# A gated hybrid decoder block on one core: gate scalings, a weight conversion, two row blocks of the output projection and one prepared product change their places

## The chip, the core and the metric

The kernel runs on one NeuronCore of a Trainium2 chip. Its engines work side by side, each on its own queue of instructions: TensorE (PE in the profile, with PEld for its weight loads), VectorE (DVE), ScalarE (ACT), GpSimd (POOL) and SyncE (SP), which here issues the DMA transfers. The metric is the time of one execution in device microseconds (us).

## The reference

One decoder layer on 1024 rows of 1024 numbers in float32, with two attention branches whose outputs are gated and added, a projection, and a gated feed-forward part:

```python
h = rmsnorm(x, mix_norm_g[l])
proj = h @ w_in[l]
qa, ka, va, q_lat, kv_lat, k_r, g_a, g_b = jnp.split(proj, IN_OFFSETS, axis=-1)
...
y = jax.nn.sigmoid(g_a) * (o_a @ w_o_swa[l]) + jax.nn.sigmoid(g_b) * (o_b @ w_o_mla[l])
x = x + y @ w_out[l]
h = rmsnorm(x, ffn_norm_g[l])
x = x + (jax.nn.silu(h @ w_gate[l]) * (h @ w_up[l])) @ w_down[l]
return rmsnorm(x, final_norm_g)
```

`o_a` comes from a sliding-window attention and `o_b` from a latent attention, each with 8 heads of 64.

## The kernel before

**Products in three parts.** Every float32 operand is split into a high part (a cast to the reduced type `fp32r`, made by ScalarE) and a low part (the difference, made by VectorE). `split` (L161) writes both. A product is then three matmuls per 128 of depth (`mm3`, L168): high by high (L172), high by low (L173), low by high (L174). So a product can begin when the cast is there, and its third matmul needs VectorE's subtraction as well.

**Seven products in place of eight.** The gate projection (`g_a`, `g_b`) and the feed-forward products are done by the class `Seven` (L710). It works through pairs `j` of weight columns; for each pair it makes seven products `q` in the order 1, 6, 2, 7, 5, 4, 3 out of sums and differences of weight quarters and of row quarters. A pair's raw weights come in two halves `kh` of the depth. For the next pair, `run` (L789) does at given products: the loads, the scaling of the gate weights by the norm's gain (`scale_part`, L739, four pieces `k` per half, done by ScalarE in `scale_gate`, L831), and the `mix` (L750), in which GpSimd makes the sums. `prep` (L764) makes the high and low part (`wl`) of a product's weights; `n_ahead` says how many products ahead of its use (3 for the gates).

**The gates run inside the sliding-window attention.** The loop at L1025 goes over 16 query blocks; each does three gate products and in between the block's transposes, scores and sums. TensorE and SyncE keep the written order there; the order of ScalarE, VectorE and GpSimd is made by a planner that runs ahead of the chip with its own picture of costs, after the written order as priority. GpSimd has the sums' denominators (`den`, L935) and the scaling of the probabilities in the same queue as the mix.

**The mixing loop** (L1444) goes over eight column tiles `dc` in the order 4, 5, 0, 1, 6, 7, 2, 3. Tile number `i` loads what later tiles need, takes the sigmoids of the next tile (L1429), and in `mix_b` (L1411) makes the product `oB` with the MLA output weights in two halves, in PSUM buffers of which there are four; VectorE multiplies each half by its gate (L1420), adds, and splits the result into `yh` and `yl`. The output weights come in pairs (`ob`, in the order 2, 0, 3, 1), each used by two tiles, and are converted by `conv_to`: pair 3 at the end of tile 2, for use in tile 4. Small SBUF tiles share 21 buffers. From L1043 up to the fourth segment of the next loop, every engine's order is the planner's.

**The output projection** (L1611) goes through four segments (`seg`) of four row blocks `b`. Each block adds 24 matmuls (8 column tiles of `y` by three) in one PSUM buffer, `xo`, and VectorE adds the result to `x`.

**Start of the feed-forward part.** From segment 3 on (L1613) the order of TensorE, VectorE, ScalarE and GpSimd is the written one. Products are called one by one (L1654 on), and between them stand `prep_to(n)`, which prepares the weights of all products before number `n`, and the late parts of the transposed rows (`rest`, L1498: casts `b22h`, `t3h`, and four subtractions).

Of the kernel before, what the change touches and what calls it, by code (L numbers as in the profile page):

```python
# [21 lines left out]
NK = D // P  # L22
# [67 lines left out]
def hybrid_block_kernel(  # L90
# [49 lines left out]
    def uid(name):  # L140
        counter[0] += 1
        return f"{name}_{counter[0]}"

    def U(name, dt=F32, shape=(P, 1024)):
        return pool.tile(list(shape), dt, tag="u", name=uid(name))
# [4 lines left out]
    def tiny(name, w=1):  # L150
        return small.tile([P, w], F32, tag=f"t{w}", name=uid(name))

    def P1(name, shape=(P, 512)):
        return ps1.tile(list(shape), F32, tag="ps", name=uid(name))

    def PX(name, shape=(P, 512)):
        return psum["x"].tile(list(shape), F32, tag="ps", name=uid(name))
# [10 lines left out]
    def mm3(ps, pairs, first=True, last=True, go_on=False):  # L168

        n = len(pairs)  # L170
        for i, ((ah, al), (bh, bl)) in enumerate(pairs):
            nc.tensor.matmul(ps, ah, bh, start=first and i == 0, stop=False, skip_group_check=go_on)  # L172
            nc.tensor.matmul(ps, ah, bl, start=False, stop=False, skip_group_check=go_on)  # L173
            nc.tensor.matmul(ps, al, bh, start=False, stop=last and i == n - 1, skip_group_check=go_on)  # L174
# [4 lines left out]
    def add(out, a, b, eng):  # L179
        eng.tensor_tensor(out, a, b, op=ALU.add)  # L180

    def blk(b, n=1):
        return slice(b * P, (b + n) * P)

    def half(s):
        return slice(512 * s, 512 * s + 512)
# [32 lines left out]
    st = Stream()  # L219
# [89 lines left out]
    def rstd_of(ss, width, r=None):  # L309
        ms = tiny("ms")  # L310
        nc.gpsimd.tensor_scalar(ms, ss, 1.0 / width, EPS, op0=ALU.mult, op1=ALU.add)  # L311
        if r is None:
            r = tiny("rstd")
        nc.gpsimd.tensor_tensor(r, ms, neg_half, op=ALU.pow)  # L314
        return r
# [6 lines left out]
    def hT(k, sl):  # L322
        hi, lo = quad[(k // 4, sl.start // 512)]
        c = slice(sl.start % 512, (sl.stop - 1) % 512 + 1)
        return hi[:, k % 4, c], lo[:, k % 4, c]

    def load_x(b):
        t = U("x")
        nc.sync.dma_start(t, x[blk(b), :])
        return t  # L330
# [188 lines left out]
    ps = kvq_ps[0] = PX("kvq")  # L519
# [334 lines left out]
        for d, t in late:  # L854
            nc.sync.dma_start(d, t)

    gates = Seven(NK, "g", load_gate, gate_done, 3, (1, 6), 5, scale=scale_gate, scale_at=[(2, 0, 0, 2), (7, 0, 2, 2), (7, 1, 0, 2), (5, 1, 2, 2)], piece=2, vec=(2, 5))

    def sw_q(it):
        qn = U("qn")  # L860
# [3 lines left out]
    for b in range(NB):  # L864
# [4 lines left out]
        ps = PX("ql", (P, 416))  # L869
# [109 lines left out]
    for i, b in enumerate((4, 5, 6, 7, 0, 1, 2, 3)):  # L979
        ps = P1("kl", (P, KVL))  # L980
# [184 lines left out]
    ob = {}  # L1165
# [110 lines left out]
    def mix_a(dc, sh, c0, n, ps=None):  # L1276
        if ps is not None:
            oa_ps[(dc, sh)] = ps
        ps = oa_ps[(dc, sh)]
        if (sh, c0) == (0, 0):  # L1280
            if dc < 4:
                ar[dc] = U("ar")
            elif dc % 2 == 0:
                t = V("ar", F32, (P, 2, S))
                ar[dc], ar[dc + 1] = t[:, 0], t[:, 1]
            if dc % 2 == 0:
                wo[dc // 2] = st.get(("oa", dc // 2))
        w = wo[dc // 2]
        mm3(ps, [((w[0][:, c, blk(dc % 2)], w[1][:, c, blk(dc % 2)]), oaT[(c, sh)]) for c in range(c0, c0 + n)],
            c0 == 0, c0 + n == 4)  # L1290
        if c0 + n == 4:
            nc.scalar.copy(ar[dc][:, half(sh)], oa_ps.pop((dc, sh)))
            if sh == 1 and dc < 4:
                nc.sync.dma_start(ar_d[dc], ar.pop(dc))
# [16 lines left out]
    DCS = (4, 5, 0, 1, 6, 7, 2, 3)  # L1311

    def load_sigs(dc):
        for i in (dc, 8 + dc):
            load_sig(i)
        if dc < 4:
            ar[dc] = U("ar")
            nc.sync.dma_start(ar[dc], ar_d[dc])
# [92 lines left out]
    def mix_b(dc, i):  # L1411
        if dc % 2 == 0:
            wo[4 + dc // 2] = st.get(("ob", dc // 2))
        w = wo[4 + dc // 2]
        ga, gb = gate.pop(dc), gate.pop(8 + dc)
        for sh in range(2):
            cs = half(sh)
            pb = PX("oB")
            mm3(pb, [((w[0][:, c, blk(dc % 2)], w[1][:, c, blk(dc % 2)]), obT[(c, sh)]) for c in range(4)])
            nc.vector.tensor_tensor(gb[:, cs], pb, gb[:, cs], op=ALU.mult)  # L1420
            if i == 7:
                add(ga[:, cs], ga[:, cs], gb[:, cs], nc.vector)
                split(*hT(dc, cs), ga[:, cs])
        for sh in range(2 if i < 7 else 0):
            cs = half(sh)
            add(ga[:, cs], ga[:, cs], gb[:, cs], nc.vector)
            split(*hT(dc, cs), ga[:, cs])

    def sigmoids(dc):  # L1429
        for i in (dc, 8 + dc):  # L1430
            sigmoid(i)
        a_ = ar.pop(dc)
        for sh in range(2):
            nc.gpsimd.tensor_tensor(gate[dc][:, half(sh)], a_[:, half(sh)], gate[dc][:, half(sh)], op=ALU.mult)
# [9 lines left out]
    for i, dc in enumerate(DCS):  # L1444
        if i in (1, 2):
            st.load_to(st.index[("ob", (3, 1)[i - 1])])
        if 2 <= i < 6:
            st.load_to(st.index[("out", 0, OUT0[i - 2])])
        if i + 2 < 8:
            load_sigs(DCS[i + 2])  # L1450
        if rest:
            mix_a(*rest.pop(0), 0, 4, PX("oA"))
        if i + 1 < 8:
            sigmoids(DCS[i + 1])
        mix_b(dc, i)
        if i in (2, 3):
            st.conv_to(st.index[("ob", (3, 1)[i - 2])])
        if i >= 4:
            st.conv_to(st.index[("out", 0, OUT0[i - 4])])

# [60 lines left out]
    def ffn_done(j, m, ps, f, sh, other):  # L1521
# [8 lines left out]
        else:  # L1530
# [3 lines left out]
    ffn = Seven(HF, "gu", load_w, ffn_done, 4, (2, 7), 5, head,  # L1534
                {(1, 6): [("load", 2, 0)], (1, 7): [("load", 2, 1)], (1, 5): [("mix", 2)]})
# [75 lines left out]
    for seg, (sh, hf) in enumerate(((0, 0), (0, 1), (1, 1), (1, 0))):  # L1611
        if seg == 3:
            in_order.__enter__()  # L1613
        if seg in (0, 1, 3):
            r = {0: 0, 1: 1, 3: 2}[seg]
            wo2 = [st.get(("out", r, j)) for j in range(4)]
        hs = half(hf)
        for b in range(4 * sh, 4 * sh + 4):
            if seg in (0, 2):
                x2[b] = load_x(b)  # L1620
            if (seg, b) == (2, 4):
                ffn.load_part(0, 0)
            if (seg, b) == (2, 6):
                ffn.load_part(0, 1)
            if (seg, b) == (2, 7):
                ffn.mix(0)
            ps = P1("xo")
            mm3(ps, [(hT(k, blk(b)), (wo2[k // 2][0][:, k % 2], wo2[k // 2][1][:, k % 2])) for k in DCS])
            add(x2[b][:, hs], ps, x2[b][:, hs], nc.vector)
            if seg in (0, 2):  # L1630
                st.conv_to(st.index[("out", seg // 2 + 1, b % 4)])
            if seg in (1, 3):
                xn = U("xn")
                ss = tiny("ss")
                nc.scalar.activation(xn, x2[b], AF.Square, accum_out=ss)  # L1635
                rs = rstd_of(ss, D)
            lower = to_h(*prev) if prev is not None else None
            prev = None
            if seg in (1, 3):
                nc.vector.scalar_tensor_tensor(xn, x2[b], rs, fg_bc, op0=ALU.mult, op1=ALU.mult)  # L1640
                prev = (xn, b)
                if (seg, b) == (3, 6):
                    ffn.prep_to(3)
                nc.sync.dma_start(x2_d[b], x2.pop(b))
            if (seg, b) == (3, 7):
                for kh in range(2):
                    ffn.load_part(1, kh)
            if lower is not None:
                if seg == 3 and b >= 6:
                    late_parts.append(lower)  # L1650
                else:
                    lower()
# [1 line left out]
    ffn.run()  # L1654
    late_parts.pop(0)()
    ffn.run()
    ffn.prep_to(4)
    late_parts.pop(0)()
    ffn.run()
    ffn.prep_to(6)  # L1660
# [89 lines left out]
    i = 0  # L1750
# [125 lines left out]
```

## Time and profile before

| | us |
|---|---|
| median of three runs | 1347.35 |
| lowest, highest | 1344.85, 1347.43 |
| the profiled execution, its own time | 1345.58 |
| its span, first to last instruction | 1343.8 |
| TensorE busy in the span | 1325.5 |
| VectorE, ScalarE, GpSimd busy | 903.5, 635.7, 567.6 |

The span is taken by the hardware profiler; the execution's time holds some 2 us around it. In the time line each row has its start, its length, engine, line, operation and the tiles written and read; in brackets stands how long the engine was idle before it, and what ended that. A row of the table of waits has the total, the number of times and the longest. A helper such as `split` or `mm3` gives all of its instructions one line, so the tiles tell them apart.

### The profile page before, as it was taken

The page shows a single profiled execution, that of the slowest core. Times are in us where ns is not written, and L with a number is a line of the kernel's source. Part 1 is how long each engine was busy: PE and PEld are TensorE (multiplying, and loading weights), DVE is VectorE, ACT ScalarE, POOL GpSimd, SP SyncE. Part 2 cuts the span into 40 slices and gives each one's busy share as a digit, 9 for nine tenths or more (in the row PEclk, how much of TensorE's full clock was granted, in tenths as well). Part 3 has the DMA queues.
Part 4 walks back from the last instruction along what each step waited for, and adds up shares of the span by engine and source line. Part 5 has one row for each costly group of instructions (what it writes and reads, how often), then busy time and mean ns, then how long its engine had stood idle before and what let it go on. Part 6 is the DMA issues. An engine that isn't in the chain of part 4 may idle for free. (4 is left out here: it accounts for less than half of the span.)

```text
span 1343.8 us, 19035 instructions
## 1 busy us (share of the span) xinstructions
PE 1325.5 (99%) x6564; PEld 1115.0 (83%) x6564; DVE 903.5 (67%) x1471; ACT 635.7 (47%) x1291; POOL 567.6 (42%) x614
## 2 busy tenths in 40 slices
PE   9999999999999999999999999999999999999997
PEld 6899878888888889877887888888888888888886
DVE  7868777776767667696458775566665664764862
ACT  7434767665556767762436223232223232644343
POOL 2116646553224554451031665756666541022521
PEclk9999999999999999999999999999999999999999
DMA  9454322335476430771432454545544425996504
GB/s 374 152 188 156 118 97 83 109 124 187 155 243 160 107 99 17 264 268 48 190 140 96 166 175 146 203 162 180 177 141 153 164 96 194 383 373 238 173 13 144
DMA packets 85311, 223.61 MB, mean 166 GB/s; under 512 B 9632, under 2 KB 16288, under 8 KB 84128
## 3 DMA queue, kind: packets, MB, share of 16 engines
q1 hardware_dynamic: 83776, 220.05, 47.5%
q10 hardware_dynamic: 1440, 2.36, 0.5%
q8 instruction: 52, 0.85, 0.3%
q14 instruction: 43, 0.35, 0.1%
HBM read 151.72 MB, written 70.12 MB: 165 GB/s over the span
## 5 line engine op out<-in xcount | busy, mean ns | idle before, releaser
L166 DVE TENSOR_TENSOR wl<-wr,wl 128x512 fp32r<-128x512 f32 x150 | 150.8, 1029 | 72.6 <-ACT wl L163 72.2
L166 DVE TENSOR_TENSOR lrv<-lr,lrv 128x1024 fp32r<-128x1024 f32 x77 | 105.1, 1396 | 49.3 <-ACT lrv L163 45.3
L163 ACT CAST lrv<-lr 128x1024 fp32r<-128x1024 f32 x77 | 80.1, 1052 | 95.7 <-PE fd L174 69.8
L172 PE MATMUL fd<-lrv 128*128 128x512 f32 x308 | 119.8, 389 | 0.0
L173 PE MATMUL fd<-lrv 128*128 128x512 f32 x308 | 119.8, 389 | 0.0
L174 PE MATMUL fd<-lrv 128*128 128x512 f32 x308 | 119.8, 389 | 0.0
L177 POOL TENSOR_TENSOR wr<-wr,sm 128x512 f32<-128x512 f32 (+1 forms) x38 | 46.2, 1225 | 145.4 <-DVE wl L166 114.2
L163 ACT CAST wl<-wr 128x512 fp32r<-128x512 f32 x150 | 86.9, 622 | 1.9 <-DVE wr L835 1.7
L1198 POOL TENSOR_TENSOR denb<-denb,neg_one 128x1 f32<-128x1 f32 x64 | 40.1, 626 | 96.2 <-ACT p L1197 84.1
L166 DVE TENSOR_TENSOR wl<-sm,wl 128x512 fp32r<-128x512 f32 x60 | 48.7, 837 | 46.3 <-ACT wl L163 46.2
L311 POOL TENSOR_SCALAR ms<-ss 128x1 f32<-128x1 f32 x32 | 9.4, 292 | 143.7 <-ACT xn L1635 67.5
L173 PEld LDWEIGHTS fd<-lrv 128*128 128x128 f32 x308 | 57.8, 188 | 12.1
L174 PEld LDWEIGHTS fd<-lrv 128*128 128x128 f32 x308 | 57.8, 188 | 12.0
L172 PEld LDWEIGHTS fd<-lrv 128*128 128x128 f32 x308 | 57.8, 188 | 11.9
L1197 ACT ACTIVATE p<-scb,nmb 128x384 f32<-128x384 f32 (+3 forms) x64 | 47.8, 747 | 33.3 <-DVE nmb L1196 25.6
L166 DVE TENSOR_TENSOR ptl<-pTb,pth 128x512 fp32r<-128x512 f32 (+2 forms) x96 | 50.5, 552 | 16.6 <-ACT pth L163 16.3
L1196 DVE CUSTOM_DVE_ANT_0 scb<-scb,mask 128x384 f32<-128x384 f32 (+3 forms) x64 | 48.6, 761 | 15.0 <-PE scb L1188 13.0
L1529 ACT ACTIVATE act<-sm 128x512 f32<-128x512 f32 x11 | 7.0, 633 | 104.8 <-DVE sm L180 104.8
L1199 POOL TENSOR_SCALAR p<-p,denb 128x384 f32<-128x384 f32 (+3 forms) x64 | 47.9, 748 | 6.3
L172 PE MATMUL xo<-wv,yh 128*128 128x512 f32 x120 | 47.4, 395 | 1.2 <-ACT yh L163 1.2
L1529 ACT ACTIVATE act<-pu 128x512 f32<-128x512 f32 x22 | 13.9, 633 | 71.0 <-DVE pu L180 71.0
L163 ACT CAST pth<-pTb 128x512 fp32r<-128x512 f32 (+2 forms) x96 | 43.4, 482 | 8.5 <-PE pTb L1213 7.5
(356 smaller groups left out, 4315.1 us busy)
## 6 DMA issues: line engine op xcount, KB each, us to landing
lr<-la_d SPq DMA_DIRECT2D x77, 256.0 KB, 5.4
wr<-in_w_gate_dram SPq DMA_DIRECT2D x22, 512.0 KB, 4.4
wr<-in_w_up_dram SPq DMA_DIRECT2D x22, 512.0 KB, 5.1
wd<-in_w_down_dram SPq DMA_DIRECT2D x22, 512.0 KB, 7.1
rb_d<-wd SPq DMA_DIRECT2D x22, 512.0 KB, 2.7
la_d<-sd SPq DMA_DIRECT2D x22, 512.0 KB, 5.9
lr<-rb_d SPq DMA_DIRECT2D x44, 256.0 KB, 5.4
lr<-in_w_down_dram SPq DMA_DIRECT2D x33, 256.0 KB, 5.4
```

Source lines behind the costliest of these rows:

```text
L163: i = nc.scalar.copy(hi, src)
L166: (eng or nc.vector).tensor_tensor(lo, src, hi.bitcast(F32), op=ALU.subtract)
L172: nc.tensor.matmul(ps, ah, bh, start=first and i == 0, stop=False, skip_group_check=go_on)
L173: nc.tensor.matmul(ps, ah, bl, start=False, stop=False, skip_group_check=go_on)
L174: nc.tensor.matmul(ps, al, bh, start=False, stop=last and i == n - 1, skip_group_check=go_on)
L177: eng.tensor_tensor(out, a, b, op=ALU.subtract)
L311: nc.gpsimd.tensor_scalar(ms, ss, 1.0 / width, EPS, op0=ALU.mult, op1=ALU.add)
L1196: nc.vector.tensor_tensor_reduce(s_, s_, m_, 1.0, -NEG, op0=ALU.add, op1=ALU.min, accum_out=nm)
L1197: nc.scalar.activation(p_, s_, AF.Exp, scale=-1.0, bias=nm, accum_out=den)
L1198: nc.gpsimd.tensor_tensor(den, den, neg_one[:, 0:1], op=ALU.pow)
L1199: nc.gpsimd.tensor_scalar(p[:, 0:w], p[:, 0:w], den, 0.0, op0=ALU.mult, op1=ALU.add)
L1529: nc.scalar.activation(dst, src, AF.Silu)
```

## The change

Four places change; no arithmetic is added or left out.

1. In the gates, the last two pieces of the next pair's first half are scaled at product 2 in place of product 7, and the last two of its second half at product 7 in place of product 5.
2. In the mixing loop, the fourth weight pair in number (`ob` 3) is converted at the end of tile 1 in place of tile 2. Pair 1 stays at the end of tile 3.
3. In the first segment of the output projection, blocks 0 and 1 get their PSUM buffers together. The first six column tiles are summed for block 0, then for block 1, then the last two for block 0, and for block 1.
4. In the feed-forward part, product 4 is prepared together with product 3, ahead of the second late part and of product 2.

```diff
-    ... scale_at=[(2, 0, 0, 2), (7, 0, 2, 2), (7, 1, 0, 2), (5, 1, 2, 2)], piece=2, vec=(2, 5))
+    ... scale_at=[(2, 0, 0, 2), (2, 0, 2, 2), (7, 1, 0, 2), (7, 1, 2, 2)], piece=2, vec=(2, 5))
...
         mix_b(dc, i)
-        if i in (2, 3):
-            st.conv_to(st.index[("ob", (3, 1)[i - 2])])
+        if i in (1, 3):
+            st.conv_to(st.index[("ob", (3, 1)[i // 2])])
...
-            ps = P1("xo")
-            mm3(ps, [(hT(k, blk(b)), (wo2[k // 2][0][:, k % 2], wo2[k // 2][1][:, k % 2])) for k in DCS])
+            if seg == 0 and b < 2:
+                if b == 0:
+                    xo2 = [P1("xo") for _ in range(2)]
+                    for ks in (DCS[:6], DCS[6:]):
+                        for u in range(2):
+                            mm3(xo2[u], [(hT(k, blk(u)), (wo2[k // 2][0][:, k % 2], wo2[k // 2][1][:, k % 2])) for k in ks],
+                                ks[0] == DCS[0], ks[0] != DCS[0])
+                ps = xo2[b]
+            else:
+                ps = P1("xo")
+                mm3(ps, [(hT(k, blk(b)), (wo2[k // 2][0][:, k % 2], wo2[k // 2][1][:, k % 2])) for k in DCS])
             add(x2[b][:, hs], ps, x2[b][:, hs], nc.vector)
...
     late_parts.pop(0)()
     ffn.run()
-    ffn.prep_to(4)
+    ffn.prep_to(5)
     late_parts.pop(0)()
     ffn.run()
     ffn.prep_to(6)
```

More of the change, by code (lines that the diff above doesn't have):

```diff
@@ L855, in gate_step @@
             nc.sync.dma_start(d, t)
-    gates = Seven(NK, "g", load_gate, gate_done, 3, (1, 6), 5, scale=scale_gate, scale_at=[(2, 0, 0, 2), (7, 0, 2, 2), (7, 1, 0, 2), (5, 1, 2, 2)], piece=2, vec=(2, 5))
+    gates = Seven(NK, "g", load_gate, gate_done, 3, (1, 6), 5, scale=scale_gate, scale_at=[(2, 0, 0, 2), (2, 0, 2, 2), (7, 1, 0, 2), (7, 1, 2, 2)], piece=2, vec=(2, 5))
     def sw_q(it):
```

## The prediction

> **What bounds the kernel now.** I read the head of the page first, then the table of TensorE's waits, then the time line around each wait.
>
> ```profile
> span 1343.8 us, 19035 instructions
> PE 1325.5 (99%) x6564; PEld 1115.0 (83%) x6564; DVE 903.5 (67%) x1471; ACT 635.7 (47%) x1291; POOL 567.6 (42%) x614
> ...
> PE fa L172 <- ACT wl L163: 3.3, 3, 1.5
> PE xo L172 <- ACT yh L163: 1.2, 1, 1.2
> ```
>
> TensorE (PE) is busy for all but 18.3 us of the span, so only its stops can give anything. The table names few: three waits of the gate and feed-forward products (`fa`) for a converted weight (`wl`), 3.3 us together, and one of the output projection (`xo`) for the mixed rows (`yh`). The time line places them, with two more on `oB`, the product with the MLA output weights. The bracket is PE's idle time and what ended it.
>
> ```profile
> 197.68 0.50 PE L172 MATMUL fa<-hh,wl 128*128 128x512 f32 x1 [1.04 <-ACT wl L163]
> ...
> 276.76 0.50 PE L172 MATMUL fa<-hh,wl 128*128 128x512 f32 x1 [0.76 <-ACT wl L163]
> ...
> 587.09 0.50 PE L172 MATMUL oB<-obT,wh 128*128 128x512 f32 x1 [0.94 <-ACT wh L163]
> ...
> 589.40 0.50 PE L174 MATMUL oB<-obT,wl 128*128 128x512 f32 x1 [0.89 <-DVE wl L166]
> ...
> 616.32 0.50 PE L172 MATMUL xo<-wv,yh 128*128 128x512 f32 x1 [1.24 <-ACT yh L163]
> ...
> 716.92 0.39 PE L174 MATMUL fa<-b21h,wl 128*128 128x512 f32 x1
> 718.77 0.50 PE L172 MATMUL fa<-b11h,wl 128*128 128x512 f32 x1 [1.46 <-ACT wl L163]
> ...
> 719.50 0.50 PE L174 MATMUL fa<-b11h,wl 128*128 128x512 f32 x1
> 719.84 0.40 PE L172 MATMUL fa<-b11h,wl 128*128 128x512 f32 x1
> ```
>
> A stop costs more than its bracket. In the last one four steps take 719.84 - 716.92 = 2.92 us. Undisturbed, matmuls of this shape start 0.227 us apart (a row quoted further down, at 727.79, is the 35th after that at 719.84), so four take 0.91 and the twelve of a product 2.72. The stop costs 2.01 us: 1.46 idle and 0.55 more, since the third matmul needs the low part that VectorE (DVE) makes after ScalarE's (ACT) cast. I put 0.55 on each stop, once on the pair at 587 and 589, where the two halves are late one after the other: 1.59 and 1.31 (gates), 2.38 (`oB`), 1.79 (`xo`), 2.01 (feed-forward). That is 9.08 us, all that this change can reach.
>
> **Gate weights.** The four scaling pieces of a gate pair's second half (`kh` 1) and the four of its first half now hang on one product each; two of each half move one product up. Nothing is added or removed: 56 scalings of one kind before and after. What must move is the cast that PE waits for at 197.68.
>
> ```profile
> 175.78 1.71 ACT L837 ACTIVATE wr<-wr,gT 128x256 f32<-128x256 f32 x4
> ...
> 181.50 0.47 ACT L933 ACTIVATE pe<-sc,nm 128x256 f32<-128x256 f32 x1 [2.97 <-DVE es L927]
> ...
> 190.32 0.62 ACT L163 CAST wl<-sm 128x512 fp32r<-128x512 f32 x1 [4.07 <-POOL sm L177]
> ...
> 197.00 0.62 ACT L163 CAST wl<-wr 128x512 fp32r<-128x512 f32 x1
> ...
> 176.77 0.74 POOL L180 TENSOR_TENSOR sm<-wr,wr 128x256 f32<-128x256 f32 x1 [0.98 <-ACT wr L837]
> 183.61 0.20 POOL L935 TENSOR_TENSOR den<-den,es 128x4 f32<-128x4 f32 x1 [6.10 <-ACT pe L933]
> 183.76 0.73 POOL L180 TENSOR_TENSOR sm<-wr,wr 128x256 f32<-128x256 f32 x1
> ```
>
> The cast at 197.00 comes late because GpSimd (POOL) mixes the next pair late: it does one addition at 176.77, then its queue holds `den`, which waits 6.10 us for the Exps, and the rest of the mix stands behind it, although its scaled inputs were done when ACT's block ended at 177.49. The sum that ACT casts at 190.32 is 4.07 us late for that, and VectorE's scores and the Exps follow late. The four scalings at 175.78 already run in one piece, the later two right behind the earlier ones, and ACT then waits 2.97 us with nothing to do. Raising the priority of two that already stand there moves nothing on ACT, and the order on POOL is not edited. Bounds: both stops go (2.90 us gained), or the pieces push other work (the slower case below). I take 0, by the row at 175.78.
>
> **Fourth output pair** (`ob` 3). One cast and one subtraction move from the end of tile 2 to the end of tile 1 of the mixing loop. Its data has long been there.
>
> ```profile
> 557.50 0.38 SPq L238 DMA_DIRECT2D wr<-in_w_o_mla_dram  x1
> wr<-in_w_o_mla_dram SPq DMA_DIRECT2D x1, 512.0 KB, 6.1
> ...
> SPq L238 <- DVE sg L180: 15.2, 3, 9.1
> ...
> 579.36 1.06 ACT L1269 ACTIVATE sg<-sg 128x1024 f32<-128x1024 f32 x1
> 585.47 0.62 ACT L163 CAST yh<-sg 128x512 fp32r<-128x512 f32 x1 [1.47 <-DVE sg L180]
> 586.00 1.04 ACT L163 CAST wh<-wr 128x1024 fp32r<-128x1024 f32 x1
> ...
> 601.90 1.27 DVE L1420 TENSOR_TENSOR sg<-oB,sg 128x512 f32<-128x512 f32 x2
> ```
>
> The load landed at 563.6 and the cast waits in line behind tile 2's `yh`. From tile 1's end it stands ahead of the sigmoid at 579.36, 6.6 us earlier; what it costs there (1.04 us on ACT, as much on VectorE) fits into gaps such as the 1.47 us before 585.47. The stop of 2.38 us goes. Late next is PSUM: `oB` has four buffers and a tile uses two. Without the stop PE is at this tile at some 586.0 (587.09 less the 0.94 and a part of the 0.55), and at the last one six halves later, at 586.0 + 6 x 2.72 = 602.3. It needs there the buffer that VectorE reads at 601.90 to 602.57. That is a stop of 0.3 us and half of 0.55 with it, 0.57 in all, so 1.81 stay. Were VectorE's row there sooner, 2.38 would; were the cast held up by a missing SBUF buffer, 0. It takes two of the 21 small ones 6.6 us sooner, and they are short here: the row of SP's queue shows weight loads that wait for VectorE to free one, 9.1 us at the longest. The loads behind it (gates, `w_out`) would each come a place later.
>
> **Two row blocks together.** 24 matmuls per block stay 48; the first 18 of block 1 move ahead of the last 6 of block 0. They need only what block 0 has used already.
>
> ```profile
> 610.16 0.39 PE L172 MATMUL xo<-wv,yh 128*128 128x512 f32 x1
> ...
> 615.65 0.62 ACT L163 CAST yh<-sg 128x512 fp32r<-128x512 f32 x1 [1.84 <-DVE sg L180]
> ...
> 616.30 0.69 DVE L166 TENSOR_TENSOR yl<-sg,yh 128x512 fp32r<-128x512 f32 x1
> ```
>
> PE would enter this stage at 610.16 - 1.81 = 608.35, do 36 matmuls (8.17 us) and come to the last tile's rows at 608.35 + 39 x 0.227 = 617.2, with the high part there from 616.27 and the low part from 616.99. The stop of 1.79 is covered, with 0.9 us to spare, and this cover is what lets the 1.81 of `oB` through: in the old order the wait would have grown by just that. The sum of block 0 is added by VectorE some 2 us later against PE's work; nobody waits for it before the next stage. I take 1.79; the bounds are 0 and 1.79.
>
> **One more product prepared** (`prep_to(5)`). One cast and one subtraction move ahead of the second late part and of product 2's Silu; all four engines run in written order here, so every delay counts.
>
> ```profile
> 716.32 1.28 ACT L1529 ACT_TABLE_LOAD   x1
> 717.61 0.60 ACT L1529 ACTIVATE act<-fa 128x512 f32<-128x512 f32 x1
> 718.11 1.13 ACT L163 CAST wl<-wr 128x512 fp32r<-128x512 f32 x2
> ...
> 722.63 0.62 ACT L163 CAST wl<-wr 128x512 fp32r<-128x512 f32 x1
> ...
> 726.44 0.69 DVE L166 TENSOR_TENSOR wl<-wr,wl 128x512 fp32r<-128x512 f32 x1
> ...
> 727.79 0.39 PE L174 MATMUL fa<-b21h,wl 128*128 128x512 f32 x1
> ...
> 714.64 1.30 POOL L177 TENSOR_TENSOR wr<-wr,sm 128x512 f32<-128x512 f32 x1 [4.63 <-DVE wl L166]
> 715.08 1.41 DVE L177 TENSOR_TENSOR t2l<-t,t2h 128x512 fp32r<-128x512 f32 x1
> ```
>
> Product 4 no longer waits behind table load and Silu, and starts 2.01 us sooner. But its partner's cast stays behind them. The subtraction put first delays the late part by 0.6 us, the Silu too, and one cast instead of two follows it: product 5's cast ends near 719.3 as before. The chain from there (transposed rows, cast of product 6 at 722.63, subtraction of product 7 at 726.44 to 727.13) doesn't move. PE now waits in product 6 for the cast that ends at 723.25 (the product began 21 steps after 719.84, at 724.61, and would begin 2.01 sooner), and in product 7, whose third matmul stood at 727.79, for the low part until 727.26 (727.13 and an estimate of 0.13 for the step from VectorE to PE and for a subtraction that ends a little later). So 0.53 less a restart step of 0.11, 0.42, is left. Bounds: 2.01 if that chain came forward too; -0.35 if the subtraction meets POOL's 1.30 us at 714.64 and ends 0.77 late. For this the row at 715.08 is the nearest: 1.41 us beside POOL, against 0.69 at 726.44. I take 0.42, as VectorE would begin at 714.48, ahead of POOL. The Trainium skill bears on it ("SBUF — State Buffer", Who interferes with whom): a VectorE instruction with two SBUF inputs and a GpSimd one that reads SBUF exclude each other for a whole instruction, and the one issued first wins. The two rows agree; by it 0.42 holds if VectorE is first, and -0.35 if POOL is.
>
> **The sum:** 0 + 1.81 + 1.79 + 0.42 = 4.02 us. The profiled execution took 1345.58, so it becomes 1341.56. The three runs shown have their median 1.77 above the profiled execution and their lowest 0.73 below. I add 0.94, half the way to the median: **1342.5**.
>
> **The rivals.** *All stops go:* the planned order of ACT and POOL changes enough that the mix is no longer split by `den`. For it: POOL sits idle for 6.10 us right there. Against: the block at 175.78. 4.02 + 2.90 = 6.92, so 1339.6.
>
> *The pair's conversion doesn't come sooner:* the order of this stage is planned, and the cast may keep its place for want of a buffer. Against: nothing but its place in line held it at 586.00. Then 1.79 + 0.42 are left, 1344.3.
>
> *Slower:* the scalings, now in blocks of four, take their place ahead of casts that PE needs next. Two of them are 0.85 us (half of 1.71), and some casts are hardly ahead of their product:
>
> ```profile
> 150.82 0.63 ACT L163 CAST wl<-sm 128x512 fp32r<-128x512 f32 x1
> ...
> 151.68 0.48 PE L172 MATMUL fa<-t1h,wl 128*128 128x512 f32 x1
> ```
>
> Here 0.23 us are left; a delay beyond that decides. At seven changes of pair 7 x (0.85 - 0.23 + 0.55) = 8.2 us are lost: 1342.5 + 8.2 = 1350.7. Against it: ACT's idle 2.97 us at 181.50, which would swallow them.
>
> **How the numbers follow.** Forecast 0.47, all stops 0.21, pair unmoved 0.18, slower 0.14. About 0.2% (2.7 us) is what a measurement of this kernel can tell from no change; faster than that is below 1344.7. The forecast's own range is 1340.5 to 1344.9. Faster: 0.42 of the forecast, 0.20 of the second, 0.07 of the third, 0.69. Same: 0.05 + 0.01 + 0.11 + 0.01 = 0.18. Slower 0.13. The range is 1337.8 (every stop gone, 9.08, is 1337.4) to 1348.5, which leaves out most of the slower case and little below.
>
> **What would show it.** Right: no wait of `oB` for `wh` or `wl`, none of `xo` for `yh`; the gate waits at 197 and 277 still there; the wait at 718.8 gone and one of about 0.7 us for product 6's cast in its place, and a short one of `oB` for VectorE's read. Wrong: gate waits gone with POOL's additions ahead of `den`; a `wh` cast still behind tile 2's `yh`; new waits of `fa` early in the gates; or new waits in the attention stage between, whose order on all engines is planned and where PE now stops for some 2 us.

## The result and the profile after

The changed kernel takes 1342.01 us (median of 7 runs, 1340.2 to 1343.51) beside 1346.97 us of the kernel before (7 runs on the same chip): a ratio of 0.997, 95% interval 0.996 to 0.998. Two later comparisons, each on another set of runs, gave 0.9966 (0.9953 to 0.9978) and 0.9964 (0.9951 to 0.9976). So the change is worth 5.0 to 5.2 us by the medians, where the prediction's sum had 4.02. One execution of a later run, that of the two row blocks alone, took 3439.43 us, without a cause on record, and is left out of its ratio.

The head of the page and the table of TensorE's waits, after:

```profile
span 1338.4 us, 19037 instructions
...
PE 1325.0 (99%) x6564; PEld 1115.5 (83%) x6564; DVE 904.0 (68%) x1471; ACT 635.5 (47%) x1291; POOL 566.9 (42%) x614
...
PE fa L172 <- ACT wl L163: 2.0, 3, 1.1
...
PE fa L172 <- ACT pu L812: 0.2, 1, 0.2
```

TensorE does the same work (1325.0 us against 1325.5) in a span that is 5.4 us shorter; its idle time fell from 18.3 to 13.4 us. The waits of `oB` and `xo` are not in the table any more; of `fa` for `wl`, two of 1.1 and 0.8 us are as before, the third, of 1.46 us ahead of product 4, is gone, and a short one has come ahead of product 6. The time line of TensorE after, at the places that the prediction showed (start, duration, then the idle time before it and what ended that):

```profile
197.61 0.50 PE L172 MATMUL fa<-hh,wl 128*128 128x512 f32 x1 [1.08 <-ACT wl L163]
...
276.66 0.50 PE L172 MATMUL fa<-hh,wl 128*128 128x512 f32 x1 [0.78 <-ACT wl L163]
...
607.43 0.39 PE L172 MATMUL xo<-wv,yh 128*128 128x512 f32 x1
...
616.27 0.39 PE L172 MATMUL xo<-wv,yh 128*128 128x512 f32 x1
...
712.61 0.39 PE L172 MATMUL fa<-b11h,wl 128*128 128x512 f32 x1
...
718.38 0.50 PE L172 MATMUL fa<-b21h,wl 128*128 128x512 f32 x1 [0.16 <-ACT wl L163]
...
721.85 0.50 PE L172 MATMUL fa<-b21h,wl 128*128 128x512 f32 x1 [0.15 <-ACT pu L812]
```

Read against the rows of before, they give a running balance of the same matmul's start. No row of `oB` has a bracket any more. The gates stand where they stood (197.61 for 197.68). The first `xo` starts at 607.43 for 610.16, 2.73 sooner, of which some 0.33 was there before the stage (the first `oB` starts at 563.91 for 564.23; most of it arises near 332 us, where profiles without the gate edit show it too); 2.40 is the pair. Behind the place of the old `xo` wait the lead has grown by 1.79. Product 4 starts at 712.61 for 718.77. Then products 6 and 7 wait, briefly by their brackets, but with the slow restart of a stop each time, and by the starts of the matmuls behind them give 1.18 back: 0.71 and 0.47. Of the 2.02 gained at product 4, 0.84 stays. 2.40 + 1.79 + 0.84 = 5.03.

### The profile page after: what moved, and what is told of

Its sections match the earlier page's. It is cut to its first block, busy times and chain, and to the rows that moved or that the text cites. A ratio compares the mean times of both kernels' runs of the same rounds, so it can differ in the third digit from the quotient of the medians.

```text
span 1338.4 us, 19037 instructions
## 1 busy us (share of the span) xinstructions
PE 1325.0 (99%) x6564; PEld 1115.5 (83%) x6564; DVE 904.0 (68%) x1471; ACT 635.5 (47%) x1291; POOL 566.9 (42%) x614
## 5 line engine op out<-in xcount | busy, mean ns | idle before, releaser
L172 PE MATMUL fb<-t2h,wl 128*128 128x512 f32 x120 | 47.4, 395 | 0.0
```

## The experiments

Ten kernels and two repeats of the changed one answer three questions: what each edit does alone, what holds the stops that stayed, and whether there is a faster version. Differences of the time line below are those of the same matmul's start in two profiles; they are finer than the times, in which executions of one kernel spread over up to 5.5 us.

### Each edit alone

**Gate scalings alone.**

```diff
-    ... scale_at=[(2, 0, 0, 2), (7, 0, 2, 2), (7, 1, 0, 2), (5, 1, 2, 2)], ...
+    ... scale_at=[(2, 0, 0, 2), (2, 0, 2, 2), (7, 1, 0, 2), (7, 1, 2, 2)], ...
```

> The kernel before with the edit to the gate scalings alone. My theory: the scalings of the pairs that stop TensorE already stand in blocks of four, so nothing moves there; the waits of `fa` for `wl` near 197.7 and 276.8 stay at about 1.0 and 0.8 us, and the time changes by 0 (within 0.5 us). Rival 1: these two stops go, 2.9 us faster. Rival 2: the scalings push casts back, new `fa` waits in the gates and some 2 to 8 us slower.

Ratio 1.0006 (0.9998 to 1.0015). TensorE's and GpSimd's time lines of this run:

```profile
198.61 0.50 PE L172 MATMUL fa<-hh,wl 128*128 128x512 f32 x1 [1.09 <-ACT wl L163]
...
277.69 0.50 PE L172 MATMUL fa<-hh,wl 128*128 128x512 f32 x1 [0.79 <-ACT wl L163]
```

```profile
177.68 0.74 POOL L180 TENSOR_TENSOR sm<-wr,wr 128x256 f32<-128x256 f32 x1 [0.95 <-ACT wr L837]
184.52 0.20 POOL L935 TENSOR_TENSOR den<-den,es 128x4 f32<-128x4 f32 x1 [6.10 <-ACT pe L933]
```

Both stops are there, to 0.05 us as long as before, and GpSimd's mix is still cut in two by `den` with its 6.10 us. Of the 56 scalings a single one changes its place (in the changed kernel from 154.5 to 153.1); the others keep theirs to 0.2 us. The edit does nothing that can be measured; rivals 1 and 2 fall.

**The pair's conversion alone.**

```diff
-        if i in (2, 3):
-            st.conv_to(st.index[("ob", (3, 1)[i - 2])])
+        if i in (1, 3):
+            st.conv_to(st.index[("ob", (3, 1)[i // 2])])
```

> The kernel before with the earlier conversion of the fourth output weight pair alone. My theory: both `oB` stops near 587 and 589 go and no stop for PSUM comes in their place (the changed kernel showed none), but without the two row blocks together the `xo` wait for `yh`, 1.24 us before, grows by just the 2.4 us saved, to about 3.6, and the next stage starts as before: 0 us. Rival: the rows of the last tile come sooner too when TensorE is sooner, since its sums are what they are made from, so the `xo` wait stays near 1.2 and 1.8 to 2.4 us are kept.

Ratio 1.0012 (1.0003 to 1.0021): not the 0 that I expected but 0.4 to 2.8 us slower. TensorE's time line, and below it the table of busy times by stretch (stretch; its length; busy us and instructions of PE, PEld, DVE, ACT and POOL; then the granted clock of TensorE, the DMA share and GB/s):

```profile
607.43 0.39 PE L172 MATMUL xo<-wv,yh 128*128 128x512 f32 x1
...
615.53 0.80 PE L172 MATMUL xo<-wv,yh 128*128 128x512 f32 x1 [3.18 <-ACT yh L163]
616.12 0.63 PE L173 MATMUL xo<-wv,yh 128*128 128x512 f32 x1
616.55 0.63 PE L174 MATMUL xo<-wv,yl 128*128 128x512 f32 x1
```

```profile
612.06:615.47 3.41, 0.29 (x2) 0.00 (x0) 2.63 (x4) 1.23 (x2) 1.56 (x1) 1.00 0.00 0
615.47:618.88 3.41, 3.35 (x8) 2.65 (x9) 2.58 (x4) 1.25 (x3) 0.00 (x0) 0.50 0.00 0
618.88:622.29 3.41, 3.41 (x17) 2.77 (x16) 1.83 (x3) 3.17 (x4) 0.00 (x0) 1.00 0.00 0
```

The `oB` stop is gone and the first `xo` stands at 607.43, just as in the changed kernel. Then the wait for the last tile's rows is 3.18 us for 1.24: they come 0.8 us sooner only, 0.3 of which was there before the stage. And behind it TensorE works at half its clock, 0.50 granted, its matmuls 0.43 us apart for 0.227, until 618.88. Against before, 2.40 are won and 3.26 lost again, a net loss of 0.9 us on the time line. The page "TensorE: Matmul & The Clock Gate" of the Trainium skill (Part 1) has such a gate: the clock halves when a window of about 3.4 us was idle, and comes back after a busy one. The trace comes near that: TensorE is idle for 3.12 of the 3.41 us ahead of the half clock, which itself lasts 3.41 us.

**The two row blocks alone** (the diff's third part, as shown above).

> The kernel before with the two row blocks summed together alone. My theory: the `xo` wait of 1.24 us goes and 1.8 us are kept up to the feed-forward stage; the `oB` waits stay at 0.94 and 0.89; 1.8 us faster. Rival: the gain is eaten in a later stage whose order is bound by another engine, 0 us.

Ratio 0.9991 (0.9983 to 1.0), so 0 to 2.3 us faster. The matmul that waited in before, block 0's first with the last tile's rows, is now the 40th of the segment; TensorE's time line:

```profile
621.00 0.39 PE L172 MATMUL xo<-wv,yh 128*128 128x512 f32 x1
```

No wait, and against before the lead grows in this segment by 1.80 us, the 1.79 expected. The next stages eat 0.17 of it; this run carries a late start and a stop of 0.40 near 153 that have nothing to do with the edit (see "A stop that comes and goes").

**The fifth product's preparation alone.**

```diff
-    ffn.prep_to(4)
+    ffn.prep_to(5)
```

> The kernel before with one more prepared product alone. My theory: the wait of 1.46 us at product 4 goes, and short waits of about 0.15 us come in products 6 and 7, whose parts stand behind the Silu chain; 0.8 us faster (0.4 to 0.9). Rival 1: the chain behind comes forward by the whole amount, 2.0 us faster. Rival 2: 0.4 us slower, with DVE's subtraction locked out by POOL.

Ratio 0.9997 (0.9988 to 1.0005). TensorE's time line:

```profile
723.94 0.50 PE L172 MATMUL fa<-b21h,wl 128*128 128x512 f32 x1 [0.39 <-ACT wl L163]
...
727.41 0.50 PE L172 MATMUL fa<-b21h,wl 128*128 128x512 f32 x1 [0.18 <-ACT pu L812]
```

Product 4 waits no more, and behind it 2.03 us are won; products 6 and 7 give 1.45 back; 0.58 is left, inside 0.4 to 0.9. Both rivals fall. How much the edit is worth depends on which two executions are compared. From the first `fa` of the feed-forward part to the 117th, the kernels with `prep_to(4)` and the late table load take 40.23 (before), 40.02, 39.99 and 39.99 (the three runs above) and 40.23 us (the next run); those with `prep_to(5)` take 39.40 (the changed kernel's first profile), 39.65 (this run), and 39.64, 39.65 and 39.66 (later runs). The means are 0.49 us apart. The 0.84 above sets the slowest of the one group against the fastest of the other.

### Pair and blocks together

The two edits above in one kernel, nothing else.

> The kernel before with the earlier pair and the two row blocks, and nothing else. My theory: alone, the pair's gain is lost again in a `xo` wait of 3.18 us and in the slow clock behind it (0.50 granted for 3 us); with the two blocks summed together there is no wait and no slow clock, so 2.4 + 1.8 = 4.2 us are kept up to the feed-forward stage. Rival, by adding the two measured alone (+0.12% and -0.09%): no change. The wait at product 4 stays at 1.2 to 1.5 us.

Ratio 0.9974 (0.9964 to 0.9984), 3.5 us faster; the two alone add up to none. On the time line the lead goes from -1.77 (a late start) to 2.44 us over both places, 4.21. The first edit makes TensorE early for rows that come hardly sooner; the second gives it other matmuls until then. ScalarE's cast of the rows, and below it TensorE:

```profile
616.97 0.62 ACT L163 CAST yh<-sg 128x512 fp32r<-128x512 f32 x1 [1.74 <-DVE sg L180]
...
618.36 0.39 PE L172 MATMUL xo<-wv,yh 128*128 128x512 f32 x1
```

The matmul that waited 1.24 us in before and 3.18 with the pair alone, now the 40th, starts here in its turn, 0.77 us after its rows are cast. These two edits are more than four fifths of the whole change by the time line (4.21 of 5.03), and two thirds by the medians (3.5 of the 5.1 of the changed kernel beside it).

### What holds the gate stops

```diff
-    gates = Seven(NK, "g", load_gate, gate_done, 3, (1, 6), 5, ...)
+    gates = Seven(NK, "g", load_gate, gate_done, 3, (1, 6), 7, ...)
```

> The changed kernel with the gates' mixing moved two products later (mix at 7 for 5), so that GpSimd does the sums for the two pairs that stop TensorE in one go instead of having them split by `den`. My theory: it is GpSimd's place behind `den` that makes both stops, so the waits of `fa` at 197 and 277 go, 2.9 us faster than the changed kernel; `den` now splits the pair behind each, which may bring a stop there. Rival: the stops come from ACT's or DVE's chain of scores and Exps, and stay (0 us); or new stops elsewhere in the gates eat it (0 or slower).

The changed kernel itself ran beside it:

> The changed kernel once more, as it is, beside the runs below: 0.3% faster than before (some 4 us), with the waits of its first profile: `fa` for `wl` near 197 and 277 (1.1 and 0.8 us), none of `oB`, none of `xo`, and about 0.15 us each in products 6 and 7 of the feed-forward stage.

(In the order 1, 6, 2, 7, 5, 4, 3 product 7 stands one place ahead of 5, so the mixing comes one product sooner; "two products later" above is a slip.) The time is 1337.24 us beside 1339.82 of the changed kernel, ratios to before 0.994 (0.9928 to 0.9953) and 0.9966 (0.9953 to 0.9978). GpSimd's time line of this run:

```profile
176.60 0.74 POOL L180 TENSOR_TENSOR sm<-wr,wr 128x256 f32<-128x256 f32 x1 [0.96 <-ACT wr L837]
...
180.33 0.74 POOL L177 TENSOR_TENSOR wr<-wr 128x256 f32<-128x256 f32 x1
183.28 0.20 POOL L935 TENSOR_TENSOR den<-den,es 128x4 f32<-128x4 f32 x1 [2.22 <-ACT pe L933]
```

and ScalarE's and TensorE's:

```profile
186.09 0.62 ACT L163 CAST wl<-sm 128x512 fp32r<-128x512 f32 x1
...
196.20 0.48 PE L172 MATMUL fa<-hh,wl 128*128 128x512 f32 x1
```

All six sums now stand in the time in which GpSimd had waited for the Exps. The cast of the sum, at 190.32 in the kernel before with 4.07 us of waiting for GpSimd, is at 186.09 without a wait, and the matmul at 196.20, the one that waited at 197.61, has no bracket. The same holds at the second place (273.81 for 276.66). The lead over the changed kernel grows by 3.16 us at the two, and no new wait of `fa` comes in the gates. So the place behind `den` made both stops: what the change needed there was an earlier mix, not earlier scalings.

### What gives the preparation's gain back

```diff
     ffn.n_ahead = 1
     ffn.run()
+    nc.scalar.activation(tiny("st"), neg_half, AF.Silu)
```

> The changed kernel with one added activation (Silu on a 128x1 tile, its output unused) ahead of ACT's 1.4 us of idle time in product 3 of the feed-forward stage, so that the 1.28 us table load stands there and not between the transposed rows and the first Silu. My theory: the load is on the chain that makes products 6 and 7 wait; the chain comes forward by some 1.3 us, both waits go, and the 1.2 us that the preparation gave back are kept: 1.2 us faster than the changed kernel. Rival: the chain is held by the subtraction beside GpSimd and by TensorE's own transposes, or the load returns (two loads), and nothing is gained, or up to 1.3 us lost.

Ratio 0.9969 (0.9956 to 0.9981), on the changed kernel's 0.9966: by the times, nothing. The profiled execution, with 1344.43 us the slowest of the six, has a stop of 1.58 us near 155 and half the clock behind it, in a stage that the edit doesn't touch; whether the five without a profile have it too isn't known, so the times alone leave the edit's worth open. At the feed-forward stage both waits are gone and the run wins 1.1 us back. ScalarE's time line there:

```profile
709.75 1.28 ACT L1664 ACT_TABLE_LOAD   x1
...
717.07 0.62 ACT L1501 CAST t3h<-t 128x512 fp32r<-128x512 f32 x1
717.59 0.60 ACT L1529 ACTIVATE act<-fa 128x512 f32<-128x512 f32 x1
718.08 0.62 ACT L163 CAST wl<-wr 128x512 fp32r<-128x512 f32 x1
```

The table load stands in idle time, there is one load as before, and the Silu follows the cast of the rows directly. So it was the load of 1.28 us, on ScalarE between the rows and the Silu, that held the casts of products 6 and 7.

### Both additions

The early mix and the early Silu in the changed kernel; then the same with `prep_to(4)`; and the changed kernel beside them.

> The changed kernel with both additions: the gates' mixing at product 7 instead of 5, and the early Silu whose output is unused. My theory: the two gains lie in different stages and add up, 3.1 us and 1.1 us by the two traces, so 4.2 us faster than the changed kernel run beside it (0.31%) and some 8 us faster than before (0.6%); no wait of `fa` is left except a possible one near 152, where ACT's scaling waits for a weight load. Rival: the later stage starts sooner against its loads, and a new wait for a DMA eats one of the two (2 to 3 us faster than the changed kernel).

> As the run with both additions, but the preparation of the fourth product fewer, as it was before the change (4 for 5). It asks whether the edit has a worth of its own once the table load is early. My theory: product 4 again waits behind the Silu, but that comes 1.3 us sooner, so the wait shrinks from 1.2 to 1.5 us to at most 0.2 and the time is within 0.5 us of the run with both. Rival: the wait of 1.2 us comes back whole, 1.8 us slower than with both.

> The changed kernel as it is, beside the two runs above: 0.3% faster than before, 4.2 us slower than with both additions.

The three took 1336.26, 1337.62 and 1341.08 us; ratios to before 0.9925 (0.9912 to 0.9938), 0.9933 (0.9921 to 0.9945) and 0.9964 (0.9951 to 0.9976). With both, 10.0 us are gone from the kernel before, nearly twice what the change alone brings, and the gains do add up: 4.8 us by the medians, and by the time line 3.16 in the gates and 1.20 in the feed-forward stage (between them 0.41 is lost against the first profile of the changed kernel, in stages that neither addition touches). TensorE's waits with both additions:

```profile
PE warm L510 <- DVE warm L507: 1.2, 1, 1.2
PE scb L1186 <- ACT p L1197: 1.1, 3, 0.6
```

`fa`, first in the table of before, is nowhere in it. Without the fifth product's preparation, product 4 stops again, for a third matmul this time:

```profile
711.49 0.50 PE L174 MATMUL fa<-b11h,wl 128*128 128x512 f32 x1 [0.26 <-DVE wl L166]
```

The bracket is 0.26 where I expected at most 0.2, and with the restart of the cast's wait before it the stage loses 0.9 us on the time line, not 0.5 or less (1.4 by the medians; the intervals overlap). The edit keeps a worth of its own; the 1.8 of the rival is not reached.

### A stop that comes and goes

Four of the fourteen profiles have a stop of `fa` near 152 to 155, of kernels whose code there is no different from the others'. ScalarE's and TensorE's time lines of the second repeat of the changed kernel, which has it:

```profile
151.96 0.91 ACT L837 ACTIVATE wr<-wr,gT 128x256 f32<-128x256 f32 x2 [5.68 <-DMA wr<-in_w_gt_dram]
...
155.47 0.50 PE L172 MATMUL fa<-t1h,wl 128*128 128x512 f32 x1 [1.12 <-ACT wl L163]
```

Two scalings wait for a weight load, with the Exps and the cast that `fa` needs behind them. In the first profile of the changed kernel the same wait is 4.17 us and ends at 147.92. To take it out, the last kernel has that half scaled by GpSimd:

```diff
         if j == 0:
             nc.vector.tensor_scalar(t[:, k], t[:, k], g, None, op0=ALU.mult)
+        elif (j, kh) == (1, 1):
+            nc.gpsimd.tensor_scalar(t[:, k], t[:, k], g, None, op0=ALU.mult)
```

> The kernel with both additions, and one half of one gate pair (j 1, `kh` 1) scaled by GpSimd instead of ScalarE. In the runs so far ScalarE's first two scalings of this half wait 3.6 to 6.1 us for the weight load, with the Exps and the next cast queued behind them; where the load is late, TensorE stops near 152 to 155 for 0.4 to 1.6 us. My theory: this wait makes part of the spread between runs of one kernel; with GpSimd, which has nothing to do there until the Exps are done, ScalarE waits for no load, the Exps start 2 us or more sooner, no stop comes near 152, and the time is 0 to 1 us below that with both additions (0.6 to 0.8% below before). Rival: GpSimd's late sums push the second pair's casts, and a new `fa` wait comes near 165 to 180; slower by 0.5 to 2 us.

GpSimd's and ScalarE's time lines (lines of code behind L836 are two higher here):

```profile
147.37 3.64 POOL L837 TENSOR_SCALAR wr<-wr,gT 128x256 f32<-128x256 f32 x4 [2.85 <-DMA wr<-in_w_gt_dram]
150.97 0.20 POOL L937 TENSOR_TENSOR den<-den,es 128x4 f32<-128x4 f32 x1
```

```profile
147.60 0.47 ACT L935 ACTIVATE pe<-sc,nm 128x256 f32<-128x256 f32 x1 [4.44 <-DVE nm L927]
```

The mechanism is as expected: the Exps wait for VectorE alone, and no `fa` waits in the gates. The time is not: 1337.03 us (1335.12 to 1337.97), ratio 0.9937 (0.9924 to 0.9951), no different from the version without it, and the spread is no smaller. That this stop makes the spread isn't shown; the executions differ also in their first 10 us, by up to 2.7 us. TensorE's first matmuls in the pair with blocks (late) and in before:

```profile
5.90 5.40 PE L522 MATMUL kvq<-wr,h 128*128 128x512 f32 x7 [1.07 <-DMA wr<-in_w_x_dram]
```

```profile
5.72 4.53 PE L522 MATMUL kvq<-wr,h 128*128 128x512 f32 x10 [1.11 <-DMA wr<-in_w_x_dram]
```

In seven of the fourteen profiles these matmuls start 0.86 us apart, twice the usual 0.43, until the record of the granted clock begins, at 9.0 to 10.3 us; in the other seven it begins at 3.9 to 6.3. That is the late start named above. In the two repeats of the changed kernel 1.96 and 2.41 us are lost by the first `fa`, of the 3.0 and 4.5 us by which their spans exceed that of the first profile.

## Why the prediction came out

**Gates, 0: right, for the reason given.** The earlier scalings left both stops as they were, and the mix behind `den` was their cause, as the run with the early mix shows. ScalarE's block of four stands at 175.70 as it stood at 175.78. The rival in which all stops go needed just what the change doesn't do.

**Pair, 1.81: the mechanism right, the size 2.40.** The cast stands ahead of the sigmoids, as ScalarE's time line after shows:

```profile
579.05 1.04 ACT L163 CAST wh<-wr 128x1024 fp32r<-128x1024 f32 x1
580.00 2.00 ACT L1269 ACTIVATE sg<-sg 128x1024 f32<-128x1024 f32 x2
```

The step that failed is the stop of 0.57 for PSUM at the last tile. I had left VectorE's read at 601.90, two in one piece; the planner moved it too. VectorE's time line after:

```profile
600.24 0.68 DVE L1420 TENSOR_TENSOR sg<-oB,sg 128x512 f32<-128x512 f32 x1
...
602.57 0.68 DVE L1420 TENSOR_TENSOR sg<-oB,sg 128x512 f32<-128x512 f32 x1
```

The first buffer is free at 600.92, ahead of TensorE, which comes to the last tile 24 matmuls before 607.43, at 602.0, and the bound "were VectorE's row there sooner, 2.38" is what came. No buffer was missing for the early cast.

**Blocks, 1.79: right** (1.79, and 1.80 alone). The rows' cast ends 0.75 us ahead of the matmul at 616.27, where I had 0.9 to spare. That this cover lets the pair's gain through was right too, and understated: in the old order the wait does not only take the 2.4 us back, it halves the clock behind it.

**Preparation, 0.42: the mechanism right, the size 0.84 in these two profiles, 0.58 alone, and 0.49 on the mean of all.** So the term was nearly right, and 0.84 is in part the luck of the two executions. The new waits are in products 6 and 7 as said, but cost 1.18 and 1.45 us where I had 1.59. Product 6's cast, which I had left in its place, ends at 718.32; against TensorE's start of the stage that is 0.40 us sooner than in before (0.16 in the run with this edit alone). Product 7 stops for ScalarE's copy of the sum out of PSUM (`pu`), not for its low part, so the 0.13 us that I had estimated for the low part, from no row, decided nothing. VectorE was first beside GpSimd, the case that 0.42 stood on: its two subtractions took 1.29 us in one piece, and GpSimd's addition beside them 1.68 for 1.30. After the change:

```profile
709.09 1.29 DVE L166 TENSOR_TENSOR wl<-wr,wl 128x512 fp32r<-128x512 f32 x2 [0.23 <-ACT wl L163]
710.30 0.69 DVE L177 TENSOR_TENSOR t<-tp,t 128x512 f32<-128x512 f32 x1
710.90 1.19 DVE L177 TENSOR_TENSOR t2l<-t,t2h 128x512 fp32r<-128x512 f32 x1
```

```profile
709.86 1.68 POOL L177 TENSOR_TENSOR wr<-wr,sm 128x512 f32<-128x512 f32 x1 [4.64 <-DVE wl L166]
```

**The sum:** 4.02 said, 5.03 on the time line, 5.0 by the medians. In these two profiles two terms were 0.59 and 0.42 too small. With the mean of all profiles for the preparation the time line gives 4.68, and the 0.3 to 0.5 us that the medians have above it aren't explained. The predicted 1342.5 lies 0.5 above the measured 1342.01, and that it lies so near is partly luck. The profiled execution came out 5.38 us below that of before, 1.36 more than the sum; the way from the profiled execution to the median, taken as 0.94, was 1.81 in the changed kernel's seven runs (1340.2 for the profiled one), 0.87 more, which hid two thirds of that.

**The slower rival** did not come. Its place with 0.23 us of margin is a real one, but what uses the margin up is a late weight load, with the gate edit and without.

**The signs.** The gate waits stayed and those of `oB`, `xo` and product 4 went, as said. The wait for product 6's cast is 0.16 us by its bracket, not 0.7 (0.71 by the starts behind it), and the short one of `oB` for VectorE's read, the sign of the 0.57, did not come.

## What to carry to other kernels

Two edits on one path are not to be priced one by one: making the matmul engine early is worth nothing, or less, until the next wait is covered with other work that is ready. Ahead of a stop, look what stands before the late operation in its engine's queue: the two cures that worked best here moved six additions ahead of a wait for another engine, and a table load into idle time. A stop's bracket understates it, by about half a microsecond at each restart here.

## What the runs showed of the hardware

A stop can cost as much by the clock behind it as by its length. TensorE's 3.18 us stop was followed by 3.41 us at 0.50 of the clock. A stop of 1.58 us, in the run with the early Silu, was followed by the same, and 1.67 us were lost by that; stretches as above, the last row from the run of pair and blocks:

```profile
152.75:156.16 3.41, 1.83 (x9) 0.99 (x8) 0.69 (x1) 3.41 (x13) 1.22 (x2) 1.00 0.00 0
156.16:159.57 3.41, 3.41 (x9) 2.64 (x10) 3.25 (x6) 2.57 (x7) 3.40 (x6) 0.50 0.20 77
159.57:162.98 3.41, 3.41 (x21) 2.94 (x19) 2.72 (x9) 0.58 (x1) 3.41 (x5) 1.00 0.32 108
...
713.39:716.80 3.41, 1.95 (x9) 1.19 (x7) 2.35 (x4) 3.38 (x5) 0.11 (x1) 1.00 0.00 0
```

The half clock began 0.9 us behind the end of that stop, not at it. In both runs it lasted 3.41 us, and the full clock ahead of it 43 times (to 156.16) and 179 times (to 615.47) that long by the clock's record: in these traces the clock changes in steps of 3.41 us. In the step ahead of the half clock TensorE was idle for 1.58 and 3.12 us.

The stops of 1.46 us (before, and pair and blocks), 1.12 and 1.09 were followed by matmuls at the usual distance; the one in the last row lies whole in one step, with TensorE busy for 1.95 of 3.41 us, and the clock stays full. The page "TensorE: Matmul & The Clock Gate" of the Trainium skill ("Why this matters for your kernels") asks for no idle time over about 3 us; here 1.58 us was enough, in a step with TensorE busy for 1.83. Whether it is the idle time of a step that counts, or also how scattered its matmuls are, and where between 1.46 and 1.58 us the bound lies, these runs don't settle.
